# The MLP of a decoder block by Strassen's algorithm, in two phases over DRAM, and an output projection with 512 columns

## The chip, the core and the metric

The kernel runs on one core of a Trainium2 chip. The metric is the device time of one execution in microseconds (us): the median of several executions. In the rows PE is TensorE (matmuls), PEld its weight loads, DVE is VectorE, ACT ScalarE, POOL GpSimd, and SP SyncE, which issues the transfers (DMA) between DRAM and the on-chip memory SBUF. Matmul results land in PSUM.

## The reference, cut to what matters

```python
def reference(x, ...):                       # x: 1024 tokens x 1024 channels, float32
    h = rmsnorm(x, norm_mix_g)
    ...                                      # attention branch y_a, state-space branch y_b
    merged = sigmoid(g_a) * y_a + sigmoid(g_b) * y_b
    x = x + merged @ w_out                   # output projection, 1024 x 1024
    h2 = rmsnorm(x, norm_mlp_g)
    x = x + square(relu(h2 @ w_up)) @ w_down # MLP, hidden width 4096
    return rmsnorm(x, norm_final_g)
```

## The kernel before, in words

Every float32 product is made of three matmuls. Each operand is split into a rounded part "hi" (a cast on ACT) and the rest "lo" (operand minus hi, a subtraction on DVE or POOL), and `mm3` (L112 to L117) adds hi by hi, lo by hi and hi by lo into one PSUM tile. The helper `weights` loads a weight tile of 128x1024 into `raw` (two buffers) and makes `w` (four buffers) of it: hi on ACT (L108), lo on DVE unless a caller names POOL (L109).

The attention, the state-space branch and the merge gates take the first part of the program. The last stage, `st3`, has three parts, and the change is in them.

- **Gates and merge.** The tiles `mT` (hi and lo of the merged channels) are made from three projections (`ps_v`).
- **Output projection.** Four column blocks `c` of 256; for each, eight blocks `b` of 128 tokens; for each, eight channel blocks of three matmuls into `ps_o`: 768 matmuls of 256 columns. DVE adds `ps_o` to the residual `xr[b]` (L960). After the fourth column block `norm2` makes `h2T`, the normalized tokens turned round by PE transposes (`pt`, L132), split in hi and lo (L133, L134) for one half of the tokens at a time.
- **MLP.** For each of 16 pairs of hidden blocks (128 wide), `up` makes the hidden values of both token halves: 24 matmuls of 512 columns into `ps_up`, then Relu on ACT (L975), square on DVE (L976), hi on ACT (L977), lo on DVE (L978). `down` then adds the pair's part to the output: for 8 token blocks and 2 column halves 6 matmuls of 512 columns into `ps_dn`, and DVE adds that to `xr` (L995). `up` of a pair is written ahead of `down` of the pair before. Hidden values never leave SBUF. That is 1536 matmuls up and 1536 down. The last token blocks are normalized with `gfin` (L1009, L1013) and stored (L1010, L1014).

All loads and stores are issued by SP in one order; within each engine instructions run in the order that the scheduler of the language set at build time. An engine waits where its next instruction waits, and a load waits for its buffer.

Of the kernel before, what the change touches and what calls it, by code (L numbers as in the profile page):

```python
# [11 lines left out]
F32 = mybir.dt.float32  # L12
# [7 lines left out]
P = 128  # L20
# [27 lines left out]
DP1, SP1, XP1, NKQ, NVV, NQT, QL = 3, 2, 2, 2, 2, 3, 1  # L48
DENSE = 'ssksmkcssscsabasbmmmm'
# [10 lines left out]
def f32(ap):  # L60
    return ap.bitcast(F32)
# [3 lines left out]
def hybrid_block(ctx: ExitStack, tc: tile.TileContext, a: dict, out: bass.AP, dbg=None):  # L65
# [10 lines left out]
    gain = cpool.tile([P, 2, KD], F32, name="gain")  # L76
# [18 lines left out]
    mg_d = [dtile([P, S], f"mg_d{i}") for i in range(16)]  # L95

# [75 lines left out]
    with ExitStack() as st1:  # L172
# [13 lines left out]
        def norm(half, xs4, each=None):  # L186
            for xb in xs4:
                rstd = rms_rows(tp, xb, hT[7][:, :, 512:1024])
                V.tensor_scalar(xb, xb, rstd, None, op0=ALU.mult)
            transpose_norm(tp, [(dps, "d", DP1)] * 3 + [(xps, "x", XP1)] * XN, xs4, gain[:, 0], [t[:, :, half * 512:half * 512 + 512] for t in hT], each)  # L190
# [679 lines left out]
    with ExitStack() as st3:  # L870
        dps = st3.enter_context(tc.tile_pool(name="dps3", bufs=4, space=PSUM))
        mpool = st3.enter_context(tc.tile_pool(name="mpool", bufs=8))
        ep = st3.enter_context(tc.tile_pool(name="ep", bufs=5))
# [3 lines left out]
        def e4(name, shape=(P, S)):  # L877
            return ep.tile(list(shape), F32, name=name, tag="e4")

# [18 lines left out]
        mT = []  # L898
        for fp in range(4):
            wg = weights(wpool, a["w_gate"][fp], S)  # L900
            wv = weights(wpool, a["w_val"][fp], S)
            wa = weights(wpool, a["w_ab"][fp], S)
            for i in range(2):
# [4 lines left out]
                m = operand(f"mT{f}")  # L908
                for h in range(2):
                    hs = slice(h * 512, h * 512 + 512)  # L910

                    def proj(w, x):
                        ps = dps.tile([P, 512], F32, name="ps_v", tag="d")
                        mm3(ps, [(w[:, 0, k * 256 + i * P:k * 256 + (i + 1) * P],
                                  w[:, 1, k * 256 + i * P:k * 256 + (i + 1) * P],
                                  x[k][:, 0, hs], x[k][:, 1, hs]) for k in range(4)])
                        return ps


                    tg = ep.tile([P, 512], F32, name="tg", tag="r", bufs=2)  # L920
                    A.activation(tg, proj(wg, yT), AF.Tanh, scale=0.25)
                    V.scalar_tensor_tensor(tg, tg, 1.0, proj(wv, yT), op0=ALU.add, op1=ALU.mult)
                    V.scalar_tensor_tensor(tb[:, hs], tb[:, hs], 1.0, tg, op0=ALU.add, op1=ALU.mult)
                    V.scalar_tensor_tensor(ta[:, hs], ta[:, hs], 1.0, proj(wa, aT), op0=ALU.add, op1=ALU.mult)
                    V.scalar_tensor_tensor(ta[:, hs], tb[:, hs], 0.25, ta[:, hs], op0=ALU.mult, op1=ALU.add)
                    A.activation(m[:, 0, hs], ta[:, hs], AF.Copy, scale=0.5)
                    V.scalar_tensor_tensor(m[:, 1, hs], ta[:, hs], 0.5, f32(m[:, 0, hs]),
                                           op0=ALU.mult, op1=ALU.subtract)
                mT.append(m)
        xr = []  # L930
        for b in range(NB):
            if b % 2 == 0:
                x2 = mpool.tile([P, 2, S], F32, name="x2", tag="m")
            xr.append(x2[:, b % 2, :])
            nc.sync.dma_start(xr[b], a["x"][b * P:(b + 1) * P, :])
        h2T = []

        def norm2(half):
            xs4 = []
            for j in range(4):  # L940
                b = half * 4 + j
                rstd = rms_rows(ep, xr[b], e4("junk").rearrange("p (e d) -> p e d", e=2))
                xs = e4("xs")
                V.tensor_scalar(xs, xr[b], rstd, None, op0=ALU.mult)
                xs4.append(xs)

            pool, tag = ((mpool, "m"), (oppool, "opT"))[half]
            h2T.append([t[:, i] for t in (pool.tile([P, 2, 2, 512], F32R, name=f"h2T{half}{k}", tag=tag) for k in range(4))
                        for i in range(2)])
            transpose_norm(ep, [(dps, "p", P3)], xs4, gain[:, 1], h2T[half])  # L950

        for c in range(4):
            ws = [weights(wpool, a["w_out"][c, j], S) for j in range(2)]
            for b in range(NB):
                bs = slice(b * P, b * P + P)
# [24 lines left out]
        def up(i):  # L980
            wa = [(weights(wpool, a["w_up"][i + j], S), actT[(i + j) % 4]) for j in range(2)]
            for h in range(2):
                for w, act in wa:
                    up_half(w, act, h)
            return [act for _, act in wa]

        def down(i, acts, last):
            ws = [weights(wpool, a["w_down"][2 * i + j], S) for j in range(2)]
            for b in range(NB):
                bs = slice(b * P, b * P + P)  # L990
                for c in range(2):
# [25 lines left out]
        for i in range(16):  # L1017
            cur = up(2 * i)
            if prev is not None:
                down(i - 1, prev, False)  # L1020
# [75 lines left out]
```

## Time and profile before

| | |
|---|---|
| median of 3 executions | 1619.19 us (1619.05 to 1619.24) |
| profiled execution | 1618.58 us |
| its span, first to last instruction | 1616.9 us |
| PE busy | 1590.8 us, 8658 instructions |
| DVE, ACT, POOL busy | 971.0, 579.7, 152.9 us |
| DRAM traffic | 104.76 MB read, 34.60 MB written |
| output projection | 806.3 to 900.6 us |
| MLP | 900.8 to 1609.4 us |

Busy is the time in which an engine ran an instruction. Matmuls are pipelined: a row of 0.39 us starts 0.23 us after the one ahead of it, so that the time that a matmul takes from the program is the distance of two starts and not its own length. The stages of the table were read from the first and last matmul of each tile name.

### The profile page before, as it was taken

What the parts mean: (1) busy time and instruction counts of PE and PEld (TensorE: products, weight loads), DVE (VectorE), ACT (ScalarE), POOL (GpSimd) and SP (SyncE); (2) the same over time, 40 slices, a digit from 0 to 9 for tenths busy, and PEclk for the clock granted to TensorE, in tenths of its full rate; (3) what the DMA queues carried; (4) which work ended last, traced back from release to release, by engine and by line L of the source; (5) the groups of instructions that cost most, each with busy time, mean ns of one, the idle gap of its engine ahead of it and who ended that gap; (6) DMA issues with size and microseconds to landing.
All of it is one profiled execution on the core that took longest, in us unless ns stands there. A gap on an engine that the chain in (4) does not pass through costs nothing.

```text
span 1616.9 us, 22652 instructions
## 1 busy us (share of the span) xinstructions
PE 1590.8 (98%) x8658; PEld 1357.0 (84%) x8658; DVE 971.0 (60%) x1901; ACT 579.7 (36%) x1241; POOL 152.9 (9%) x254
## 2 busy tenths in 40 slices
PE   7999999999999999999999999999999999999998
PEld 5789899888888888888899888888888888888886
DVE  7995977278888887655523554444444544544446
ACT  6344443367677676522202422222211111111222
POOL 3123544210100000000000000000000000000001
PEclk9999999999999999999999999999999999999999
DMA  6335365632122111833331111111111111011102
GB/s 230 124 106 177 113 203 155 207 101 59 56 84 87 50 50 47 289 107 109 102 120 53 40 52 53 53 53 47 45 41 51 53 52 52 29 51 52 53 27 104
DMA packets 81980, 142.93 MB, mean 88 GB/s; under 512 B 12112, under 2 KB 46928, under 8 KB 81872
## 3 DMA queue, kind: packets, MB, share of 16 engines
q1 hardware_dynamic: 81872, 141.49, 27.3%
q8 instruction: 68, 1.11, 0.3%
q14 instruction: 40, 0.33, 0.1%
HBM read 104.76 MB, written 34.60 MB: 86 GB/s over the span
## 4 chain that ended last, share of the span: by engine, by line
PE 91%; DVE 6%; issue 1%; ACT 1%; DVEq 0%; POOLq 0%; ACTq 0%
PE ps_m L147 10%; PE ps_up L115 7%; PE ps_up L117 7%; PE ps_up L116 7%; PE ps_dn L115 7%; PE ps_dn L116 7%; PE ps_dn L117 7%; PE s_ps L760 4%; PE pt L801 4%; PE ps_v L117 3%; PE ps_v L115 3%; PE ps_v L116 3%; PE o_ps L711 2%; PE o_ps L712 2%; PE ps_o L117 2%; PE ps_o L116 2%
## 5 line engine op out<-in xcount | busy, mean ns | idle before, releaser
L995 DVE TENSOR_TENSOR x<-x,ps_dn 128x512 f32<-128x512 f32 x256 | 174.7, 687 | 132.5 <-PE ps_dn L117 132.4
L108 ACT CAST w<-raw 128x1024 fp32r<-128x1024 f32 (+1 forms) x114 | 118.0, 1050 | 343.3 <-PE ps_dn L117 266.1
L147 PE MATMUL ps_m<-hT,w 128*128 128x512 f32 x768 | 215.1, 400 | 0.4 <-ACT mst L153 0.3
L115 PE MATMUL ps_up<-h2T,w 128*128 128x512 f32 x512 | 201.0, 393 | 0.9 <-ACT h2T L133 0.9
L116 PE MATMUL ps_up<-h2T,w 128*128 128x512 f32 x512 | 200.6, 392 | 0.0
L117 PE MATMUL ps_up<-h2T,w 128*128 128x512 f32 x512 | 200.1, 393 | 0.0
L116 PE MATMUL ps_dn<-w,actT 128*128 128x512 f32 x512 | 199.7, 390 | 0.0
L115 PE MATMUL ps_dn<-w,actT 128*128 128x512 f32 x512 | 199.6, 390 | 0.0
L117 PE MATMUL ps_dn<-w,actT 128*128 128x512 f32 x512 | 199.4, 390 | 0.0
L976 DVE TENSOR_TENSOR r<-r 128x512 f32<-128x512 f32 x64 | 44.3, 692 | 194.2 <-ACT r L975 194.1
L147 PEld LDWEIGHTS ps_m<-hT,w 128*128 128x128 f32 x768 | 130.6, 188 | 21.5 <-ACT mst L153 0.8
L109 DVE TENSOR_TENSOR w<-raw,w 128x1024 fp32r<-128x1024 f32 x87 | 105.0, 1221 | 25.5 <-ACT w L108 25.5
L975 ACT ACTIVATE r<-ps_up 128x512 f32<-128x512 f32 x64 | 38.2, 598 | 225.2 <-PE ps_up L117 224.1
L115 PEld LDWEIGHTS ps_up<-h2T,w 128*128 128x128 f32 x512 | 96.1, 188 | 22.3 <-ACT h2T L133 1.2
L116 PEld LDWEIGHTS ps_up<-h2T,w 128*128 128x128 f32 x512 | 96.2, 188 | 21.5
L117 PEld LDWEIGHTS ps_up<-h2T,w 128*128 128x128 f32 x512 | 95.9, 188 | 21.6
L115 PEld LDWEIGHTS ps_dn<-w,actT 128*128 128x128 f32 x512 | 96.1, 188 | 20.6
L117 PEld LDWEIGHTS ps_dn<-w,actT 128*128 128x128 f32 x512 | 96.1, 188 | 20.4
L116 PEld LDWEIGHTS ps_dn<-w,actT 128*128 128x128 f32 x512 | 96.1, 188 | 20.2
L124 POOL TENSOR_TENSOR rstd<-ss,neghalf 128x1 f32<-128x1 f32 x23 | 12.6, 550 | 993.3 <-DVE ss L122 993.3
L766 ACT ACTIVATE p<-s_ps,sst 128x640 f32<-128x640 f32 (+7 forms) x128 | 90.1, 707 | 23.5 <-PE pt L801 13.4
L109 POOL TENSOR_TENSOR w<-raw,w 128x1024 fp32r<-128x1024 f32 (+1 forms) x27 | 71.3, 2643 | 162.5 <-ACT w L108 162.5
(1383 smaller groups left out, 3293.9 us busy)
## 6 DMA issues: line engine op xcount, KB each, us to landing
raw<-w_up SPq DMA_DIRECT2D x32, 512.0 KB
raw<-w_down SPq DMA_DIRECT2D x32, 512.0 KB
raw<-w_mg SPq DMA_DIRECT2D x16, 512.0 KB
mg_d<-mst SPq DMA_DIRECT2D x32, 256.0 KB
qT<-q_d SPq DMA_DIRECT2D x16, 384.0 KB
xb<-x SPq DMA_DIRECT2D x8, 512.0 KB
w1r<-w_c SPq DMA_DIRECT2D x16, 256.0 KB
q_d<-qTs SPq DMA_DIRECT2D x16, 256.0 KB
```

What stands on the lines that cost most here:

```text
L108: (hi or A.copy)(w[:, 0, :], raw)
L109: (lo or V.tensor_tensor)(w[:, 1, :], raw, f32(w[:, 0, :]), op=ALU.subtract)
L115: T.matmul(ps, lhsT=wh, rhs=xh, start=first and i == 0, stop=False)
L116: T.matmul(ps, lhsT=wl, rhs=xh, start=False, stop=False)
L117: T.matmul(ps, lhsT=wh, rhs=xl, start=False, stop=last and i == n - 1)
L147: m = T.matmul(ps, lhsT=w[:, e, ks], rhs=hT[k][:, r, hs], start=k == 0 and i == 0, stop=k == KD - 1 and i == 2)
L760: T.matmul(s_ps[:, o:o + hi - lo], lhsT=qT[:, 2 + hp * 2 + j, :], rhs=kT[g, br, hf][:, e, lo - hf * 512:hi - hf * 512], start=e == 0, stop ...
L766: A.activation(pp[j][:, 0:w], row, AF.Exp, scale=-1.0, bias=st[:, 0, j:j + 1], accum_out=st[:, 2, j:j + 1])
L801: T.transpose(pt[:, i, j, :], c[hp, br][j][:, (i0 + i) * P:(i0 + i + 1) * P], ident)
L975: A.activation(r, ps, AF.Relu)
L976: V.tensor_tensor(r, r, r, op=ALU.mult)
L995: V.tensor_tensor(xr[b][:, cs], xr[b][:, cs], ps, op=ALU.add)
```

## The change

The two products of the MLP are made by Strassen's algorithm in the form with 7 block products and 15 block sums in place of 8 block products. For a product of a 2x2 arrangement of blocks A with one of blocks B, sums S1 to S4 of A's blocks and T1 to T4 of B's are made, seven products of them, and the results are sums of those.

- **Output projection**: two column blocks of 512, 384 matmuls of 512 columns into `ps_o`.
- **norm2** now runs for one block of 128 tokens at a time after the second column block: `xs` is the row times rstd and gain (`gm`, L977), transposed into `pt`, copied to `hb`, and turned into the operands B11 and B21 (tokens 0 to 511) or B22, T1 and T2 (tokens 512 to 1023) with their hi and lo (L969, L998, L1001). `x` after the projection goes to DRAM (`x_d`). T3 and T4 are made later from whole tiles (`late_operands`: three subtractions each in `tt`, two buffers, L1011 to L1013; lo on POOL).
- **Up phase**: 16 steps `q`, each with the weights of a pair of hidden blocks. Four weight sums `sa`, `sb` (L1067 to L1071) and three weight tiles split with lo on POOL; 7 products of 12 matmuls into `pa`, `pb`, `pc`. The two products that need no weight sum (`up_open`) of the first three steps are put ahead. The squared blocks and their sums (`e1`, `e2`, `ts`) are stored to `act_d`, 1.75 MiB for a step.
- **Down phase**: seven products `op`, each over 16 `q`. For each (op, q) a part of `act_d` (one load for two q) and a block of `w_down` (or a sum T of blocks) are split (two casts on ACT, one lo on POOL and one on DVE) and multiplied by 12 matmuls, summed over q in four PSUM tiles. `x_d` is loaded back to add to.

In total 1344 matmuls up and 1344 down, each of 512 columns.

```diff
+        def norm2(b):
+            js = slice(b % 4 * P, b % 4 * P + P)
+            xs = e4("xs")
+            rstd = rms_rows(ep, xr[b], xs.rearrange("p (e d) -> p e d", e=2))
+            V.scalar_tensor_tensor(xs, xr[b], rstd, gm, op0=ALU.mult, op1=ALU.mult)
+            nc.sync.dma_start(x_d[b], xr[b])
+            hb = e4("hb", (P, 2, 4, P))
...
+                    T.transpose(pt[:, k, :], xs[:, (kh * 4 + k) * P:(kh * 4 + k + 1) * P], ident)
+                A.copy(hb[:, kh], pt)
+            if b < 4:
...
+                split_to("B11", js, hb[:, 0])
+                split_to("B21", js, hb[:, 1], G)
+                return
...
+            t1 = hb[:, 0]
+            for e in range(2):
+                V.tensor_tensor(t1, t1, f32(ops_["B11"][e][:, :, js]), op=ALU.subtract)
+            split_to("B22", js, hb[:, 1], G)
+            split_to("T1", js, t1)
+            V.tensor_tensor(hb[:, 1], hb[:, 1], t1, op=ALU.subtract)
+            split_to("T2", js, hb[:, 1])
+        def late_operands():
...
+            for k in range(4):
+                for name, x, y, eng in (("T3", "T2", "B11", V), ("T4", "B21", "T2", V)):
...
+                    t = s4("tt", (P, 512))
+                    eng.tensor_tensor(t, xh, yh, op=ALU.subtract)
+                    eng.tensor_tensor(t, t, xl, op=ALU.add)
+                    eng.tensor_tensor(t, t, yl, op=ALU.subtract)
+                    h, l = ops_[name]
+                    A.copy(h[:, k], t)
+                    G.tensor_tensor(l[:, k], t, f32(h[:, k]), op=ALU.subtract)
...
+        def up_open(q, raw0):
+            w = weights(wpool, None, S, lo=G.tensor_tensor, raw=raw0)
+            pa, pb = acc("pa"), acc("pb")
+            e1 = e4("e1", (P, 2, 512))
+            prod(pa, w[:, :, 0:512], "B11", True)
+            A.copy(e1[:, 0], pa)
+            prod(pb, w[:, :, 512:1024], "B21", True)
+            V.tensor_tensor(e1[:, 0], e1[:, 0], pb, op=ALU.add)
+            square(e1[:, 0])
+            return pa, e1
+        def up_rest(q, raw0, raw1, pa, e1):
...
+            V.tensor_tensor(s1, a21, a22, op=ALU.add)
+            V.tensor_tensor(s2, s1, a11, op=ALU.subtract)
+            wa = weights(wpool, None, S, lo=G.tensor_tensor, raw=sa)
+            V.tensor_tensor(s3, a11, a21, op=ALU.subtract)
+            V.tensor_tensor(s4_, a12, s2, op=ALU.subtract)
+            wb = weights(wpool, None, S, lo=G.tensor_tensor, raw=sb)
+            wc = weights(wpool, None, 512, lo=G.tensor_tensor, raw=a22)
+            e2 = e4("e2", (P, 2, 512))
+            pc = acc("pc")
+            prod(pa, wa[:, :, 0:512], "T2", False)
+            A.copy(e2[:, 0], pa)
+            prod(pc, wa[:, :, 512:1024], "T1", True)
+            A.copy(e2[:, 1], pc)
+            prod(pa, wb[:, :, 0:512], "T3", False)
+            V.tensor_tensor(e2[:, 1], e2[:, 1], pa, op=ALU.add)
+            square(e2[:, 1])
+            prod(pc, wb[:, :, 512:1024], "B22", False)
+            V.tensor_tensor(e2[:, 0], e2[:, 0], pc, op=ALU.add)
+            square(e2[:, 0])
+            prod(pa, wc, "T4", False)
...
+            nc.sync.dma_start(d[:, 0:2, q % 2], e1)
+            nc.sync.dma_start(d[:, 2, q % 2], e2[:, 1])
+            nc.sync.dma_start(d[:, 3:7, q % 2], t)
...
+        opened = [up_open(q, up_raw(2 * q)) for q in range(NOPEN)]
+        late_operands()
+        for q in range(16):
+            raw0, raw1 = up_raw(2 * q), up_raw(2 * q + 1)
+            up_rest(q, raw0, raw1, *(opened[q] if q < NOPEN else up_open(q, raw0)))
...
+        def down(n, op, group, first, rhs, dst):
...
+            for q in range(16):
+                if q % 2 == 0:
+                    raw = wpool.tile([P, 2, 512], F32, name="raw", tag="raw", bufs=nbuf[0])
+                    nc.sync.dma_start(raw, act_d[q // 2][:, op])
+                t = rhs(q)
+                w = wpool.tile([P, 2, 2, 512], F32R, name="w", tag="w", bufs=nbuf[1])
+                A.copy(w[:, 0, 0], raw[:, q % 2])
+                G.tensor_tensor(w[:, 0, 1], raw[:, q % 2], f32(w[:, 0, 0]), op=ALU.subtract)
+                A.copy(w[:, 1, 0], t)
+                V.tensor_tensor(w[:, 1, 1], t, f32(w[:, 1, 0]), op=ALU.subtract)
...
+        def rhs_t2(q):
+            x, t, b22 = xy[q // 2][:, q % 2, 0], xy[q // 2][:, q % 2, 1], zload(q, 1, 1)
+            V.tensor_tensor(t, b22, t, op=ALU.subtract)
+            V.tensor_tensor(x, t, x, op=ALU.subtract)
+            return t
...
+        down(0, A11, 0, True, rhs_b11, (0, c1))
+        down(1, S1, 1, True, rhs_t1, (1, c2))
+        down(2, S2, 0, False, rhs_t2, (0, c2))
+        down(3, S4, 1, False, lambda q: z[q // 4][:, q % 4], (0, c2))
+        down(4, S3, 0, False, lambda q: xy[q // 2][:, q % 2, 0], (1, c2))
+        down(5, A12, 1, True, lambda q: zload(q, 1, 0), (0, c1))
+        down(6, A22, 0, False, rhs_t4, (1, c1))
```

DVE at the start of the MLP, before: the splits of the second token half (`h2T`, L134) stand between the squares and lo parts of the first hidden blocks.

```order
L944 TENSOR_SCALAR xs<-x_9078,rstd 128x1024
L976 TENSOR_TENSOR r<-r 128x512 x2
L134 SCALAR_TENSOR_TENSOR h2T_10077<-pt,gain,h2T_10077 128x512 x2
L134 SCALAR_TENSOR_TENSOR h2T_10078<-pt,gain,h2T_10078 128x512 x2
L134 SCALAR_TENSOR_TENSOR h2T_10079<-pt,gain,h2T_10079 128x512 x2
L134 SCALAR_TENSOR_TENSOR h2T_10080<-pt,gain,h2T_10080 128x512
L978 TENSOR_TENSOR actT_10139<-r,actT_10139 128x512
```

DVE at the same place in the changed kernel, first at the second token half: T_9605 is T1's lo, T_9607 T2's lo, B_9394 and B_9395 B11's hi and lo, x_9272 the last token block's rows.

```order
L1035 TENSOR_TENSOR x_9272<-x_9272,ps_o 128x512
L998 TENSOR_TENSOR hb<-hb,B_9394 128x512
L998 TENSOR_TENSOR hb<-hb,B_9395 128x512
L125 TENSOR_SCALAR ss<-ss 128x1
L977 SCALAR_TENSOR_TENSOR xs<-x_9217,rstd,gm 128x1024
L969 TENSOR_TENSOR T_9605<-hb,T_9604 128x4x128
L1001 TENSOR_TENSOR hb<-hb 128x512
L969 TENSOR_TENSOR T_9607<-hb,T_9606 128x4x128
```

The last addition of the projection stands ahead of all work on tokens 512 to 1023, and of each of the four blocks five such operations are made. At the end of that work come the 24 subtractions of `late_operands`, of which these are the last, and then the first weight sums:

```order
L1011 TENSOR_TENSOR tt<-T_9606,B_9394 128x512
L1012 TENSOR_TENSOR tt<-tt,T_9607 128x512
L1011 TENSOR_TENSOR tt<-B_9396,T_9606 128x512
L1013 TENSOR_TENSOR tt<-tt,B_9395 128x512
L1012 TENSOR_TENSOR tt<-tt,B_9397 128x512
L1013 TENSOR_TENSOR tt<-tt,T_9607 128x512
L1067 TENSOR_TENSOR sa<-raw 128x512
L1068 TENSOR_TENSOR sa<-sa,raw 128x512
L1070 TENSOR_TENSOR sb<-raw 128x512
L1071 TENSOR_TENSOR sb<-raw,sa 128x512
```

So `sa`, from which the weights of the first product with T2 are made, stands behind all of T1 to T4. On PE the matmuls between the last `ps_o` and that product are the 72 of the three opened steps, with 32 transposes among them.

SP's transfers before, in the MLP: loads of weights alone, in pairs.

```order
L965 DMA gfin<-g_fin 128x1024
L102 DMA raw<-w_up 128x1024 x2
L102 DMA raw<-w_down 128x1024 x2
L102 DMA raw<-w_up 128x1024 x2
L102 DMA raw<-w_down 128x1024 x2
```

SP's transfers in the changed kernel where the up phase ends: act_d_161 to act_d_168 are the eight pairs of steps, of which the first down product reads one for two `q`. First from the second pair on:

```order
L1138 DMA raw<-act_d_162 128x1024
L1117 DMA gfin<-g_fin 128x1024
L1178 DMA xy<-w_down 128x512 x6
L1138 DMA raw<-act_d_163 128x1024
L1178 DMA xy<-w_down 128x512 x3
L1097 DMA act_d_168<-e_11845 128x512
L1178 DMA xy<-w_down 128x512 x5
L1115 DMA y_11923<-x_d_153 128x1024
```

Seven more loads of `x_d` follow, and behind them:

```order
L1138 DMA raw<-act_d_164 128x1024
L1098 DMA act_d_168<-ts 128x4x512
L1178 DMA xy<-w_down 128x512 x5
L1138 DMA raw<-act_d_165 128x1024
L1178 DMA xy<-w_down 128x512 x13
L1178 DMA z<-w_down 128x512 x13
L1138 DMA raw<-act_d_166 128x1024
L1178 DMA z<-w_down 128x512 x3
L1138 DMA raw<-act_d_167 128x1024
```

The loads of `act_d`, which the running product needs one after the other, stand among loads that the second and the third product or the end of the phase need: 4 MiB of `x_d` ahead of act_d_164, and 26 blocks of `w_down` (0.25 MiB each) between act_d_165 and act_d_166.

## Rows read from the trace of the kernel before

**Rows 1.** The page: span, busy time and instructions, and the chain's shares.

```profile
span 1616.9 us, 22652 instructions
PE 1590.8 (98%) x8658; PEld 1357.0 (84%) x8658; DVE 971.0 (60%) x1901; ACT 579.7 (36%) x1241; POOL 152.9 (9%) x254
PE 91%; DVE 6%; issue 1%; ACT 1%; DVEq 0%; POOLq 0%; ACTq 0%
```

**Rows 2.** Windows of the MLP: stretch, length, busy (count) by engine, clock, DMA.

```profile
1100.00:1200.00 100.00, 100.00 (x439) 82.21 (x439) 47.75 (x64) 20.30 (x28) 0.00 (x0) 1.00 0.17 53
1300.00:1400.00 100.00, 100.00 (x440) 82.13 (x439) 48.70 (x66) 19.14 (x27) 0.00 (x0) 1.00 0.17 53
```

**Rows 3.** Timeline of PE in the output projection: start, us, engine, line, operation.

```profile
829.77 0.28 PE L117 MATMUL ps_o<-w,mT 128*128 128x256 f32 x1
...
831.55 0.28 PE L117 MATMUL ps_o<-w,mT 128*128 128x256 f32 x1
```

**Rows 4.** Timeline of PE around the start of the MLP.

```profile
900.76 0.39 PE L115 MATMUL ps_up<-h2T,w 128*128 128x512 f32 x1
...
915.20 0.50 PE L115 MATMUL ps_up<-h2T,w 128*128 128x512 f32 x1 [0.94 <-ACT h2T L133]
...
920.35 1.47 PE L132 MATMUL pt<-ident,xs 128*128 128x128 f32 x12
921.58 0.48 PE L117 MATMUL ps_up<-h2T,w 128*128 128x512 f32 x1
```

**Rows 5.** Groups by line and form: busy, mean ns, idle time ahead and its releasers.

```profile
L109 DVE TENSOR_TENSOR w<-raw,w 128x1024 fp32r<-128x1024 f32 x87 | 105.0, 1221 | 25.5 <-ACT w L108 25.5
L108 ACT CAST w<-raw 128x1024 fp32r<-128x1024 f32 x110 | 113.6, 1048 | 343.3 <-PE ps_dn L117 266.1 <-PE ps_o L117 52.4 <-DMA raw<-w_out 10.6
L109 POOL TENSOR_TENSOR w<-raw,w 128x1024 fp32r<-128x1024 f32 x23 | 58.7, 2554 | 139.0 <-ACT w L108 139.0
L733 POOL TENSOR_TENSOR pc<-pc,st 128x256 f32<-128x256 f32 x16 | 9.8, 613 | 1.2
L976 DVE TENSOR_TENSOR r<-r 128x512 f32<-128x512 f32 x64 | 44.3, 692 | 194.2 <-ACT r L975 194.1
L977 ACT CAST actT<-r 128x512 fp32r<-128x512 f32 x64 | 39.6, 621 | 21.4 <-DVE r L976 21.2
L1013 DVE SCALAR_TENSOR_TENSOR x<-x,rstd,gfin 128x1024 f32<-128x1024 f32 x7 | 9.0, 1279 | 0.0
```

**Rows 6.** Timeline of POOL, then of DVE, in the same stretch.

```profile
61.95 4.68 POOL L109 TENSOR_TENSOR w<-raw,w 128x1024 fp32r<-128x1024 f32 x1 [32.49 <-ACT w L108]
67.41 2.49 POOL L109 TENSOR_TENSOR w<-raw,w 128x1024 fp32r<-128x1024 f32 x1 [0.78 <-ACT w L108]
...
62.41 0.68 DVE L254 TENSOR_TENSOR bt__632<-bXY,fim 128x512 f32<-128x512 f32 x1
63.02 0.75 DVE L494 TENSOR_TENSOR vv<-vv,vt 128x576 f32<-128x576 f32 x1
63.68 0.68 DVE L254 TENSOR_TENSOR B<-B,bt__632 128x512 f32<-128x512 f32 x1
64.40 3.23 DVE L505 TENSOR_TENSOR wq<-B,pi 128x512 f32<-128x512 f32 x1
67.66 2.79 DVE L506 TENSOR_TENSOR wq<-wq,wq 128x512 f32<-128x512 f32 x1
```

**Rows 7.** Windows with heavy transfers (the last two columns: DMA share, GB/s).

```profile
12.00:16.00 4.00, 3.79 (x15) 2.76 (x14) 3.84 (x6) 3.86 (x7) 2.87 (x1) 1.00 1.03 411
655.00:685.00 30.00, 30.00 (x131) 24.34 (x130) 22.69 (x17) 17.34 (x15) 0.00 (x0) 1.00 0.91 321
```

**Rows 8.** Timeline of PE after its first idle time, then windows behind its last matmul.

```profile
13.75 0.80 PE L115 MATMUL ps_u<-hT,w 128*128 128x512 f32 x1
14.34 0.63 PE L116 MATMUL ps_u<-hT,w 128*128 128x512 f32 x1
14.76 0.57 PE L115 MATMUL ps_u<-hT,w 128*128 128x512 f32 x1
15.17 0.39 PE L117 MATMUL ps_u<-hT,w 128*128 128x512 f32 x1
15.40 0.39 PE L115 MATMUL ps_u<-hT,w 128*128 128x512 f32 x1
...
1609.40:1612.00 2.60, 0.00 (x0) 0.00 (x0) 2.16 (x4) 1.21 (x4) 0.69 (x2) 1.00 0.46 186
1613.00:1614.00 1.00, 0.00 (x0) 0.00 (x0) 0.73 (x2) 0.00 (x0) 0.00 (x0) 0.50 0.46 184
```

More of the change, by code (lines that the diff above doesn't have):

```diff
@@ L95, in hybrid_block @@
     mg_d = [dtile([P, S], f"mg_d{i}") for i in range(16)]
+    x_d = [dtile([P, D], f"x_d{b}") for b in range(NB)]
+    act_d = [dtile([P, 7, 2, 512], f"act_d{i}") for i in range(8)]
     def operand(name):
@@ L897, in hybrid_block @@
             aT.append(o)
-        mT = []
+        mT = [[oppool.tile([P, 2, 2, 512], F32R, name=f"mT{h}{k}", tag="opT") for k in range(4)] for h in range(2)]
         for fp in range(4):
@@ L1016, in hybrid_block, with op2 @@
-        prev = None
[L1017 to L1020, printed above, removed]
-            prev = cur
-        down(15, prev, True)
+                    ssm_part(i, h)
+                    if fp < 3:
+                        attn_part(i, h)
+            if fp == 3:
+                for i in range(2):
+                    for h in range(2):
+                        attn_part(i, h)
+        ops_ = {}
+        def op2(name, pool, tag):
+            ops_[name] = [pool.tile([P, 4, 512], F32R, name=f"{name}{e}", tag=tag) for e in range(2)]
@@ new lines, in prod @@
+        def prod(ps, w, name, first):
+            h, l = ops_[name]
+            for k in range(4):
+                ks = slice(k * P, k * P + P)
+                for i, (e, x) in enumerate(((0, h), (1, h), (0, l))):
+                    T.matmul(ps, lhsT=w[:, e, ks], rhs=x[:, k], start=first and k + i == 0, stop=k == 3 and i == 2,
+                             skip_group_check=not first)
+        def up_open(q, raw0):
[8 more added lines that the diff above has]
+            return pa, e1
@@ new lines, in hybrid_block, with mms @@
+        gfin = e4("gfin")
+        nc.sync.dma_start(gfin, a["g_fin"])
+        A11, A12, A22, S1, S2, S3, S4 = range(7)
+        xy, z = [], []
+        groups = ([acc(f"pg{i}") for i in range(4)],
+                  [acc("pg4"), dps.tile([P, 512], F32, name="pg5", tag="p", bufs=2),
+                   dps.tile([P, 512], F32, name="pg6", tag="p", bufs=2), mps.tile([P, 512], F32, name="pg7", tag="d")])
+        c1, c2 = slice(0, 512), slice(512, 1024)
+        def down(n, op, group, first, rhs, dst):
+            ps = groups[group]
+            held = []
+            def mms(q, w, b):
+                bs = slice(b * P, b * P + P)
+                for i, (e, r) in enumerate(((0, 0), (1, 0), (0, 1))):
+                    T.matmul(ps[b], lhsT=w[:, 0, e, bs], rhs=w[:, 1, r], start=first and q + i == 0,
+                             stop=q == 15 and i == 2, skip_group_check=not first)
+            for q in range(16):
[8 more added lines that the diff above has]
+                V.tensor_tensor(w[:, 1, 1], t, f32(w[:, 1, 0]), op=ALU.subtract)
+                if n == 6 and q >= 12:
+                    held.append((q, w))
+                    continue
+                for b in range(4):
+                    mms(q, w, b)
+            r, cs = dst
+            for b in range(4):
+                for q, w in held:
+                    mms(q, w, b)
+                yb = y[r * 4 + b][:, cs]
+                V.tensor_tensor(yb, yb, ps[b], op=ALU.add)
+                if n >= 5:
+                    final(r * 4 + b, cs)
```

234 lines of the change are left out of this document (134 added, 100 removed).

## The prediction

> **What bounds the kernel now.** I read the page first: PE is busy for 1590.8 of 1616.9 us and holds 91% of the chain of work that ended last, so time comes out only where PE has less to do, and goes in only where PE is made to wait [rows 1]. Then the windows of the MLP: 100 us hold 439 or 440 matmuls of 512 columns, PE is busy in all of it, DVE for about 48 us, ACT for 20, POOL for nothing, and transfers move 53 GB/s [rows 2]. One such matmul is therefore worth 100/439.5 = 0.2275 us of the program, and everything else in the MLP has slack today. Last the timeline of PE where the MLP starts: it waited 0.94 us there once, for the split of the second token half, and twelve transposes took 1.23 us, 0.10 each [rows 4]. The other engines had no work that PE had to stand for.
>
> **The change, part by part.** The sum is made against the profiled execution of 1618.6 us; the median is 0.6 above that.
>
> *Products of the MLP.* 3072 matmuls become 2688 of the same shape: 384 x 0.2275 = 87.4 us less (87.3 to 87.5 by the two windows).
>
> *Output projection.* In the timeline 15 starts of 256 columns lie 1.78 us apart, 0.1187 us each [rows 3]: 768 x 0.1187 = 91.2 us. Of 512 columns there are 384, at 0.2275 87.4 us: 3.8 us less. The transposes are 64 in both.
>
> *Start of the MLP.* Before's own wait of 0.94 us goes. What comes is a wait for DVE. By the order, after DVE's last addition of `ps_o` and up to the second weight sum of `sa`, from which the first product with T2 is made, DVE has 52 operations of 128x512, 3 squares of that size and 3 of 128x1024 (rows times rstd and gain). By the nearest groups, 692 ns and 1279 ns [rows 5], that is 55 x 0.69 + 3 x 1.28 = 41.8 us; back to back such operations start some 0.64 apart (63.02 to 63.68 was 0.66 [rows 6]), which makes it 39. The cast of `sa` on ACT (1.05) is behind them; its lo on POOL (2.55) is wanted only one matmul later [rows 5]: 3.6 more. PE has in this time 72 opened matmuls and 32 transposes: 72 x 0.2275 + 32 x 0.10 = 19.6 us. PE so stands for 39 + 3.6 - 19.6 = 23 us if nothing disturbs DVE.
>
> Something does. In one stretch of an earlier stage POOL's subtraction of 128x1024 took 4.68 us in place of 2.4 while three DVE operations of 0.68 to 0.75 ran, then DVE's next one took 3.23 us, until POOL was done, and the one after it 2.79 beside POOL's next of 2.49. From 61.95 to 70.45, 8.5 us, the two did work that alone takes about 2 x 2.4 for POOL and 5 x 0.7 for DVE, 8.3: they took turns [rows 6]. In the MLP before, POOL has no work [rows 2], so that DVE never paid for this; now it has. At the start POOL makes the lo of B22 in four pieces and of T3 and T4 in eight, each of 512 elements a row. No row has that size; it lies between 0.61 us for 256 and 2.55 for 1024 [rows 5], and I take half of the latter: 12 x 1.28 = 15.3, and two or three weight lo's of 2.55 fall in as well, 5: 20 us, which DVE loses. Without turns the wait is 23, with all of them 43, and if DVE also sits through the way from rstd to the transposes and back for a block or two, 50. I take **43**, since the rows show turns wherever both ran.
>
> [...]
>
> *Up phase, steady.* A step is 84 matmuls, 19.1 us. DVE has 15 operations of 0.69 in it, 10.4; POOL three lo's of 2.55 and one of 1.28, 8.9; ACT three casts of 1.05 and a few of 0.62, 6.2; transfers 2.75 MiB. [...] I take no wait here, and keep the other for a rival.
>
> *End of up, start of down.* SP's transfers run one behind the other at about 0.37 MiB/us (388 GB/s, between 411 and 321 [rows 7]). Each (op, q) gives PE 12 matmuls, 2.73 us. The first `xy` tiles lie where B22 lay, which is read until one product ahead of the end of the up phase. From there 9.25 MiB stand ahead of act_d_164 (1.5 of `xy`, gfin, two parts of act_d, 4 MiB of `x_d`, the last stores, 2 more of `xy`): 25 us, against six `q` and the last product and its lead, 16.4 + 4.6: a wait of 4. To act_d_165 it is 2.75 MiB, 7.4 us against two `q` of 5.5: 2. To act_d_166 it is 7 MiB, 18.9 against 5.5: 13.4. Together **19**; at 411 GB/s (0.392 MiB/us) 16.5, at 321 (0.306) 30.
>
> *Down phase, steady.* DVE has one to three operations for a (op, q) and POOL one: 1.28 + 0.69 = 2.0 in turns, and in the product with T2 1.28 + 3 x 0.69 = 3.35 against 2.73. That is 0.62 x 16 = 10 too much, of which four `w` buffers filled ahead take some 7: **3** (0 to 10). The tail behind the last matmul is the same chain of square, rstd, scaling and store as before: nothing.
>
> *Clock.* [...] And at the program's start the first matmuls after idle time lay 0.59, 0.42 and 0.41 us apart, then 0.23 [rows 8]. The four long waits above will each be followed by some work at about half rate. One costs at least 0 and by that start, 0.7 for three matmuls and something for the transposes ahead of them, up to 4. I take 1.5 each: **6** (0 to 16).
>
> The sum: 1618.6 - 87.4 - 3.8 - 0.9 + 43 + 19 + 3 + 6 = 1597.5, and 0.6 for the median: **1598 us**.
>
> **Rivals.**
> - *Waits are covered* (DVE and POOL hardly take turns in these instructions, and transfers go at 411 GB/s): 23 at the start, 16.5 at the transition, none in down, no clock: 1618.6 - 92.1 + 39.5 + 0.6 = 1567. For it: POOL's rows in turns are of 1024 elements, and there were only a few. Against: every pair that met shows it. Chance 0.22.
> - *The up phase loops on DVE and POOL*: all 15 operations take turns, and waits between them make a step 20.1 in place of 19.1: 16 more, 1614; with slow transfers (30) up to 1622. For it: 19.3 against 19.1. Chance 0.18.
> - *Slower*: POOL's subtraction of 128x512, which no row has, costs what one of 128x1024 costs, 2.4. Then a (op, q) of down needs 2.4 + 0.69 = 3.1 in turns, 0.37 over PE's 2.73, 112 times: 41 more, 1639. It decides from (1619.2 - 1598)/112 = 0.19 over, that is POOL at 2.23. Against: POOL's time falls with the size, 0.61 for 256 elements, so that 512 should stand near 1.25 [rows 5]. Chance 0.09.
> - That the change doesn't save the matmuls is no case for me: the new ones have the shape of the old, and the number is fixed by the program.
>
> The forecast, waits of 85 down to 60 us in all, 1588 to 1612, has the remaining 0.51.
>
> **How the numbers follow.** A difference of 0.2%, 3.2 us, is about what a measurement of this kernel can tell from no change. The forecast and the covered case are faster (0.73); of the up-phase case 0.11 is faster and 0.07 the same; the last is slower, 0.09. The range leaves out a part of the covered case and the slower one: 1566 to 1626.
>
> **What would show it.** Right: PE's windows in the up phase full but for its start, with the first T2 product some 60 us after the last `ps_o`; DVE operations of 2 us and more beside POOL's; gaps of PE on `act_d` loads behind the first eight `q` of down, the longest ahead of q 10. Wrong: POOL at 1.2 us with DVE at 0.69 beside it (then 1567), or PE windows of under 95 in the middle of up or down (then 1614 and more), or no gap at the transition, if the transfers were begun earlier than I let them.

## The result, and the profile after

The changed kernel takes 1640.49 us (median of four, 1637.73 to 1641.72) against 1619.2: a ratio of 1.0129, 95% interval 1.0112 to 1.0147. It is slower by 1.3%, above the range of the prediction. The profiled execution is the 1637.73 one; before's was 1618.58.

The page after, as in [rows 1] (span, busy, chain):

```profile
span 1636.0 us, 22261 instructions
PE 1527.2 (93%) x7890; PEld 1276.1 (78%) x7890; DVE 1135.0 (69%) x1927; ACT 678.9 (42%) x1443; POOL 487.5 (30%) x446
PE 66%; DVE 17%; DMA 9%; issue 3%; ACT 2%; POOL 1%; SPq 1%; DVEq 0%; POOLq 0%; ACTq 0%
```

PE has 768 instructions less and is busy for 63.6 us less, but its share of the chain fell from 91% to 66%: DVE (17%) and transfers (9%) now set part of the end. Three groups by tile give the stages, each with its first and last start; `pg` are the sums of the down phase:

```profile
L120 PE MATMUL ps_o<-w,mT x128: 389/393/480, 806.9 to 898.6; 128*128 128x512 f32 x128
L1045 PE MATMUL pa<-T,w x576: 387/393/796, 960.3 to 1291.5; 128*128 128x512 f32 x192
L1132 PE MATMUL pg<-w x1344: 387/389/796, 1292.9 to 1625.7; 128*128 128x512 f32 x192
```

And windows of the three stages, as in [rows 2]:

```profile
898.90:960.30 61.40, 23.69 (x105) 18.71 (x103) 48.91 (x61) 22.41 (x39) 24.62 (x18) 0.70 0.11 34
960.30:1291.70 331.40, 308.70 (x1272) 245.65 (x1272) 237.94 (x224) 88.72 (x122) 149.38 (x63) 0.96 0.41 138
1292.90:1627.10 334.20, 313.07 (x1344) 253.69 (x1344) 224.34 (x234) 135.71 (x252) 156.94 (x116) 0.97 0.46 157
```

Against the work of PE in each, by the prediction's own prices: the **start** took 61.4 us, of which 19.6 are matmuls and transposes: 42 lost. The **up phase** took 332.6 (960.3 to the first `pg` at 1292.9) for 1344 - 72 = 1272 matmuls, 1272 x 0.2275 = 289.4: 43 lost. The **down phase** took 333.0 for 1344, at 0.2267 (794 in 180 us of its undisturbed part) 304.7: 28 lost. The tail behind the last matmul is 10.1 us in place of 7.5. The waits of PE (total, times, longest):

```profile
PE pa L1045 <- ACT w L111: 29.0, 1, 29.0
PE pa L1045 <- DVE e L1081: 21.5, 11, 3.1
PE pg L1132 <- ACT w L1141: 17.0, 3, 12.3
...
PE pt L983 <- DVE xs L977: 7.6, 2, 5.9
PE pg L1132 <- DVE w L1144: 2.4, 1, 2.4
```

Of these rows the first and the fourth are the start, the third and the fifth the transition. The second came 11 times, in nearly every step of the up phase, and is the one that the prediction did not have. The chain of one such step, in order of time:

```profile
1104.19 0.37 SPq L1098
...
1104.66 6.50 DMA raw<-w_up
...
1111.86 0.69 DVE sb L1070
...
1113.79 0.69 DVE e L1081
1114.48 0.02 issue
1114.51 2.78 DVE e L1061
1117.29 0.61 DVE e L1084
...
1117.92 2.18 DVE e L1061
...
1120.82 1.70 DVE ts L1093
...
1123.12 2.83 DVE e L1088
...
1125.98 0.70 DVE ts L1094
...
1126.69 0.37 SPq L1098
...
1127.17 6.51 DMA raw<-w_up
```

It is a loop that never passes PE. DVE ends the last sum in `ts`; SP issues its store (L1098) and only then the load of the next weights, which it has behind the store in its order; the load lands 6.5 us later; DVE, which waited for it (5.77 us in the timeline, ahead of `sa`), makes the weight sums, then the addition from `pa` (L1081) that PE waits for, then squares and sums up to `ts`. From 1104.66 to 1127.17 it is 22.5 us, against 19.1 of matmuls. For the 13 steps behind the three opened ones that would be 13 x 3.4 = 44 us, as much as the whole loss of the up phase; the first experiment shows how much of it the loop really costs. Behind five of the eleven waits (2.35, 2.41, 2.45, 2.45 and 3.05 us) the twelve matmuls that follow take 4.2 to 4.5 us at a mean clock of 0.62 to 0.66; behind the other six (0.96 to 2.46 us) they take 2.9 at 1.00. PE's windows around the one of 2.45 us in this step (busy, clock, transfers):

```profile
1112.00:1113.00 1.00, 0.07 (x1) 1.00 0.00 0
1113.00:1114.00 1.00, 0.00 (x0) 1.00 0.00 0
...
1115.00:1116.00 1.00, 1.00 (x4) 0.50 0.74 262
1116.00:1117.00 1.00, 1.00 (x3) 0.50 0.62 238
```

The granted clock is 0.50 behind the wait, but since the chain of the loop has no row of PE, that should cost nothing more here (argued from the chain; no run kept PE busy through the wait). At the transition PE's timeline has the waits one by one:

```profile
1292.90 8.89 PE L1132 MATMUL pg<-w 128*128 128x512 f32 x38 [1.00 <-ACT w L1143]
1304.19 8.01 PE L1132 MATMUL pg<-w 128*128 128x512 f32 x34 [2.40 <-DVE w L1144]
1316.50 7.17 PE L1132 MATMUL pg<-w 128*128 128x512 f32 x24 [4.30 <-ACT w L1141]
1324.03 1.21 PE L1132 MATMUL pg<-w 128*128 128x512 f32 x4 [0.36 <-ACT w L1141]
1325.93 4.84 PE L1132 MATMUL pg<-w 128*128 128x512 f32 x20 [0.69 <-POOL w L1142]
1343.07 2.50 PE L1132 MATMUL pg<-w 128*128 128x512 f32 x5 [12.30 <-ACT w L1141]
```

The groups ahead of 1316.50 hold 38 + 34 = 72 matmuls, six `q`: that is the wait for act_d_164. Behind it come 24, 4 and 20, four more, so that the last is the wait for act_d_166.

### The profile page after: what moved, and what is told of

Read it like the earlier page. It is cut to its first block, busy times and chain, and to the rows that moved or that the text cites. A ratio compares the mean times of both kernels' runs of the same rounds, so it can differ in the third digit from the quotient of the medians.

```text
span 1636.0 us, 22261 instructions
## 1 busy us (share of the span) xinstructions
PE 1527.2 (93%) x7890; PEld 1276.1 (78%) x7890; DVE 1135.0 (69%) x1927; ACT 678.9 (42%) x1443; POOL 487.5 (30%) x446
## 4 chain that ended last, share of the span: by engine, by line
PE 66%; DVE 17%; DMA 9%; issue 3%; ACT 2%; POOL 1%; SPq 1%; DVEq 0%; POOLq 0%; ACTq 0%
PE pg L1132 17%; PE ps_m L150 10%; DMA raw<-w_up 5%; PE s_ps L763 4%; PE pt L804 4%; DVE e L1061 3%; PE ps_v L120 3%; PE ps_v L118 3%; PE ps_v L119 3%; PE o_ps L714 2%; PE pa L1045 2%; PE o_ps L715 2%; DMA xy<-w_down 2%; PE ps_o L120 2%; PE ps_o L118 2%
## 5 line engine op out<-in xcount | busy, mean ns | idle before, releaser
L1132 PE MATMUL pg<-w 128*128 128x512 f32 x1344 | 313.1, 394 | 21.1 <-ACT w L1141 17.0
L1132 PEld LDWEIGHTS pg<-w 128*128 128x128 f32 x1344 | 253.7, 190 | 80.5 <-ACT w L1141 18.2
L1142 POOL TENSOR_TENSOR w<-raw,w 128x512 fp32r<-128x512 f32 x112 | 155.7, 1393 | 179.3 <-ACT w L1141 179.3
L1045 PE MATMUL pa<-T,w 128*128 128x512 f32 x576 | 152.8, 417 | 51.7 <-ACT w L111 29.0
L112 POOL TENSOR_TENSOR w<-raw,w 128x1024 fp32r<-128x1024 f32 (+2 forms) x59 | 141.8, 2411 | 172.2 <-ACT w L111 172.2
L1045 PEld LDWEIGHTS pa<-T,w 128*128 128x128 f32 x576 | 114.2, 200 | 83.9 <-ACT w L111 29.4
L150 PEld LDWEIGHTS ps_m<-hT,w 128*128 128x128 f32 x768 | 130.6, 188 | 21.5 <-ACT mst L156 0.8
L1144 DVE TENSOR_TENSOR w<-xy,w 128x512 fp32r<-128x512 f32 x64 | 71.4, 1124 | 63.6 <-ACT w L1143 54.1
L111 ACT CAST w<-raw 128x1024 fp32r<-128x1024 f32 (+2 forms) x82 | 79.0, 967 | 51.4 <-DMA raw<-w_out 15.7
L769 ACT ACTIVATE p<-s_ps,sst 128x640 f32<-128x640 f32 (+7 forms) x128 | 90.1, 708 | 23.5 <-PE pt L804 13.4
L763 PE MATMUL s_ps<-kT,qT 128*128 128x512 f32 (+3 forms) x384 | 85.8, 337 | 0.2
L804 PE MATMUL pt<-ident,p 128*128 128x128 f32 x528 | 83.8, 275 | 2.1 <-DVE pl__5079 L708 0.9
L766 DVE CUSTOM_DVE_ANT_0 s_ps<-s_ps,cmask 128x256 f32<-128x256 f32 (+7 forms) x96 | 63.9, 677 | 19.6 <-PE s_ps L763 19.1
L1061 DVE SCALAR_TENSOR_TENSOR e<-e 128x512 f32<-128x512 f32 x48 | 75.2, 1566 | 1.4
L119 PE MATMUL ps_a<-w,hT 128*128 128x256 f32 (+1 forms) x256 | 74.7, 292 | 0.0
L118 PE MATMUL ps_a<-w,hT 128*128 128x256 f32 (+1 forms) x256 | 74.5, 291 | 0.0
L120 PE MATMUL ps_a<-w,hT 128*128 128x256 f32 (+1 forms) x256 | 74.0, 289 | 0.0
```

The costliest lines, as they stand in the source:

```text
L118: T.matmul(ps, lhsT=wh, rhs=xh, start=first and i == 0, stop=False)
L119: T.matmul(ps, lhsT=wl, rhs=xh, start=False, stop=False)
L120: T.matmul(ps, lhsT=wh, rhs=xl, start=False, stop=last and i == n - 1)
L150: m = T.matmul(ps, lhsT=w[:, e, ks], rhs=hT[k][:, r, hs], start=k == 0 and i == 0, stop=k == KD - 1 and i == 2)
L763: T.matmul(s_ps[:, o:o + hi - lo], lhsT=qT[:, 2 + hp * 2 + j, :], rhs=kT[g, br, hf][:, e, lo - hf * 512:hi - hf * 512], start=e == 0, stop ...
L804: T.transpose(pt[:, i, j, :], c[hp, br][j][:, (i0 + i) * P:(i0 + i + 1) * P], ident)
```

## The experiments

Nine kernels, of which seven have a single execution and the last two, with all or most of the edits, the median of four. The last `ps_o` starts at 898.5 to 901.3 us in them, up to 2.8 us apart though nothing ahead of the MLP was changed, so gains are read from the stage concerned and not from the total alone. First the up phase. **The stores on ACT:**

```diff
-            nc.sync.dma_start(d[:, 0:2, q % 2], e1)
+            nc.scalar.dma_start(d[:, 0:2, q % 2], e1)
...
-            nc.sync.dma_start(d[:, 3:7, q % 2], t)
+            nc.scalar.dma_start(d[:, 3:7, q % 2], t)
```

> The changed kernel, with the 48 stores to act_d issued by ACT in place of SP. Theory (queue order): in the up phase the weight sums wait for w_up loads that SP issues only after the store of ts, 1 MiB, and that land 6.5 us after it; a step is 22.5 us by that loop. With the stores elsewhere the loads go out as soon as their buffer is free: a step of about 19.1 to 19.6 us, PE's waits on the addition from pa (21.5 us) gone, and with them most of the time at the lower clock; up phase from the first T2 product on 331 down to 290 to 300, in all about 1600. Rival (turns alone): DVE and POOL are the loop, whatever the loads do: step 22 us, in all 1633 to 1640.

Measured 1606.42 us, a little above the 1600 of the theory: the up phase took 300.4 us in place of 332.6. A window of it:

```profile
1060.00:1080.00 20.00, 20.00 (x88) 16.21 (x87) 16.32 (x17) 6.01 (x9) 9.18 (x4) 1.00 0.48 169
```

PE is full, its wait for L1081 is gone, and yet DVE is still busy for 16.3 of the 20 us, and for 226 us of the phase against 238 before: the turns are there but no longer on the path. Queue order holds; turns alone fall. The run also says how much of the 43 us was the loop: 32. Most of the other 11 stay with PE full: the matmuls of the up phase start 0.2316 us apart in this window, not 0.2275, which is 5 us over 1272 (why is open), and the first 24 with T1 and T2, behind the long wait of the start, take 9.8 us in place of 5.6. **POOL's lo parts out of the up phase:**

```diff
+        def lo_copy(o, r, h, op):
+            A.copy(o, r)
...
-            w = weights(wpool, None, S, lo=G.tensor_tensor, raw=raw0)
+            w = weights(wpool, None, S, lo=lo_copy, raw=raw0)
```

(and the same for `wa`, `wb`, `wc`.)

> The changed kernel, with the lo parts of the up phase's weights not computed by POOL's subtraction but filled by a copy on ACT (part of the product is so left out: lo is not operand minus hi). POOL then has nothing to do in the steady up phase, and DVE no turns to take. Theory (one loop, of queue order and turns): DVE's stretch from the addition from pa to the last sum, 12.9 us, falls to about 6 to 7, the loop from 22.5 to below PE's 19.1, so that this too brings the up phase from 331 to 290 to 300 and the whole to about 1600. Rival (the loads' 6.5 us behind the store alone, or the transfers' volume): step stays 21 to 22.5, in all 1630 or more. Rival (ACT becomes the bound with 3.7 us more of copies): step above 20.

Measured 1600.62 us, up phase 296.5. The stores were still on SP. What changed on DVE, first in the changed kernel, then here (mean ns of one):

```profile
L1061 DVE SCALAR_TENSOR_TENSOR e<-e 128x512 f32<-128x512 f32 x48 | 75.2, 1566 | 1.4
L1091 DVE TENSOR_TENSOR ts<-e 128x512 f32<-128x512 f32 x16 | 30.5, 1908 | 0.5
L1081 DVE TENSOR_TENSOR e<-e,pa 128x512 f32<-128x512 f32 x16 | 10.9, 682 | 5.9 <-PE pa L1045 5.9
```

```profile
L1064 DVE SCALAR_TENSOR_TENSOR e<-e 128x512 f32<-128x512 f32 x48 | 34.2, 713 | 1.1
L1094 DVE TENSOR_TENSOR ts<-e 128x512 f32<-128x512 f32 x16 | 12.1, 759 | 0.4
```

The square (L1061, here L1064) went from 1566 to 713 ns, the first sum of `ts` from 1908 to 759, and DVE's busy time in the phase from 238 to 147 us: 5.7 us for each of 16 steps. Taken from a loop of 22.5 that would leave 16.8, an estimate, below PE's 19.1. But the run does not show that this alone frees PE, because SP's order came out another way at build time. In the changed kernel both loads of a step stand behind the store of `ts`; here one of them stands ahead of both stores:

```profile
1066.98 0.33 SPq L105 DMA_DIRECT2D raw<-w_up  x1
1070.55 0.37 SPq L1099 DMA_DIRECT2D act_d<-e  x1
1072.36 0.37 SPq L1101 DMA_DIRECT2D act_d<-ts  x1
1073.73 0.34 SPq L105 DMA_DIRECT2D raw<-w_up  x1
```

In every step of the phase at least one load has come ahead of the store of `ts`, and on DVE the next step's weight sum starts at 1070.44, ahead of the last sum of `ts` at 1071.64. So the loop is open in its order as well as shorter. The kernel with the stores on ACT shows that the order alone is enough; that the turns alone are enough is not shown.

The start. **The subtractions for T3 and T4 behind the first weight sums:**

```diff
-        late_operands()
...
             wc = weights(wpool, None, 512, lo=G.tensor_tensor, raw=a22)
+            if q == 0:
+                late_operands()
```

> The changed kernel, with the 24 subtractions for T3 and T4 written behind the weight sums and splits of the first step in place of ahead of them. Theory (DVE's order at the start of the MLP makes the wait of 42 us): by DVE's order 28 operations of 0.66, 3 of 1.28 and some 8 us of turns stand before the first T product now, 30 to 34 us against PE's 19.6: a wait of 11 to 15, and later one of about 15 for T3; in all 1638 - 16 = about 1622. Rival (the wait is for the loads of the first weights or for POOL's lo's, not for these subtractions): no change, 1636 to 1640.

Measured 1636.52 us: by the total no change, as the rival had it, but not for its reason. The first product with T2 now starts 41.6 us after the last `ps_o` in place of 61.5, 20 us sooner, with one with T1 ahead of it; but the phase from there to the first `pg` grew from 332.6 to 347.6. PE's waits say where it went:

```profile
PE pt L983 <- DVE xs L977: 13.6, 2, 8.8
PE pa L1045 <- ACT T L1015: 11.2, 3, 4.6
PE pa L1045 <- POOL T L1016: 1.8, 3, 0.6
```

PE now stands for T3 and T4 themselves. The order only chooses which product waits; the work on DVE and POOL between the last `ps_o` and T4 is what costs. **POOL's part in it:**

```diff
-            (lo or V).tensor_tensor(l[:, :, js], src, f32(h[:, :, js]), op=ALU.subtract)
+            if lo is None:
+                V.tensor_tensor(l[:, :, js], src, f32(h[:, :, js]), op=ALU.subtract)
+            else:
+                A.copy(l[:, :, js], src)
...
-                    G.tensor_tensor(l[:, k], t, f32(h[:, k]), op=ALU.subtract)
+                    A.copy(l[:, k], t)
```

> Stores on ACT, and the lo parts that POOL makes at the start of the MLP (B21, B22, T3, T4) filled by a copy on ACT in place of POOL's subtraction (lo is so not operand minus hi there; part of the product is left out). Theory of the prediction (20 of the 42 us of the wait are turns of DVE and POOL): wait down to about 22, in all 1586. Rival (turns are a smaller part, waits for POOL's results through the two tt buffers and the chain from rstd to xs the rest; DVE's own work in that stretch, 48.9 us busy of 61.4, is most of it): wait 28 to 36, in all 1592 to 1600.

Measured 1591.04 us against 1606.42 of the kernel with the same stores. The first T product starts 47.6 us after the last `ps_o` in place of 61.4. The window, as above:

```profile
899.79:947.35 47.56, 24.07 (x106) 19.12 (x104) 42.36 (x61) 29.01 (x51) 7.02 (x6) 0.73 0.13 45
```

The twelve lo parts of this stretch are so worth 14 us. The prediction had 15.3 for them; the other 5 of its 20 are weight lo's, which POOL still makes in this run (its 7.0 us are three of these and three rstd). A wait of 28 is left, at the rival's edge, and that is the prediction's 23 and 5. What was taken away is only half turns: DVE's busy time fell from 48.9 to 42.4, 6.5 us, and its idle time from 12.5 to 5.2, 7.3 us, much of it the waits for POOL's results through `tt` (four waits for L1016 of 1.15 to 1.43 us, 4.9 in all, in the changed kernel). **Fewer subtractions** (T2 - B11 is B22 - B12):

```diff
+            t3 = s4("t3", (P, 4, P))
+            V.tensor_tensor(t3, hb[:, 1], t1, op=ALU.subtract)
+            split_to("T3", js, t3, G)
             for e in range(2):
                 V.tensor_tensor(t1, t1, f32(ops_["B11"][e][:, :, js]), op=ALU.subtract)
...
+            t4 = s4("t4", (P, 4, P))
+            V.tensor_tensor(t4, f32(ops_["B21"][0][:, :, js]), hb[:, 1], op=ALU.subtract)
+            V.tensor_tensor(t4, t4, f32(ops_["B21"][1][:, :, js]), op=ALU.add)
+            split_to("T4", js, t4, G)
...
-        late_operands()
```

> The kernel with the stores on ACT, and T3 computed as B22 - B12, which it equals, and T4 as B21 - T2, both for each block of 128 tokens in norm2 from the float32 tile: 4 + 8 operations of 128x512 on DVE in place of 24, none of them behind the two tt buffers that wait for POOL. Theory (the wait of 42 us at the start is DVE's and POOL's work in turns): 12 operations of 0.66 and the 4 x 2.2 us that DVE waited for POOL and took turns fall away: 42 to about 26, in all 1588 to 1594. Rival (as with the moved subtractions, where the wait only went to another place): less than 6 off, 1600 or more.

Measured 1594.06 us, 12.4 below the kernel with the stores on ACT and at the upper end of what was expected; the start took 48.8 us in place of 61.4, which leaves a wait of 29 where 26 was expected. Work taken away shortens it, where work moved did not.

The transition. **More buffers for act_d, x_d written later:**

```diff
-                    raw = wpool.tile([P, 2, 512], F32, name="raw", tag="raw", bufs=nbuf[0])
+                    if q % 6 == 0:
+                        raw = wpool.tile([P, 2, 512], F32, name="raw", tag="raw", bufs=nbuf[0])
+                    else:
+                        raw = e4("raw", (P, 2, 512))
...
+                if n == 0 and q == 10:
+                    for i in range(4):
+                        y2 = mpool.tile([P, 2, S], F32, name="y2", tag="m")
```

> The changed kernel, with the act_d loads of the down phase in up to six buffers (the four free ones of e1's pool beside the two) in place of two, and the loads of x_d written in the middle of the first down product in place of ahead of it. Theory (transfers wanted later stand ahead of act_d loads on SP): the first act_d loads now go out ahead of most of them, and the loss of 28 us at the transition falls to 5 to 12: in all 1615 to 1622. Rival (the transition is limited by the volume that the first product needs, 8 MiB and the last stores): loss stays above 20, in all 1630 or more.

Measured 1635.05 us, a miss for the theory in size: the down phase itself took 325.5 us, 7.5 less, but began with a wait of 3.45. Its longest wait, 9.0 us at 1339, is again for an act_d load, behind these transfers on SP (start, time of the whole group):

```profile
1332.85 8.39 SPq L1182 DMA_DIRECT2D z<-w_down  x12
1341.58 1.73 SPq L1142 DMA_DIRECT2D raw<-act_d  x3
```

The loads of `x_d` had gone out early all the same: SP issued the eight from 1301.68 on, 4 us behind the first matmul of the phase (1297.67), and q 10, at which they are written, starts at 1327.34. Six buffers did not settle volume against order. **Later loads held back** (each behind a one-column copy that waits for the running product's `w`; on the kernel with the stores on ACT):

```diff
+        def ahead(n, q, w1):
+            if n == 0:
+                t = xy[q // 2][:, q % 2, 1]
+                A.copy(t[:, 0:1], w1)
+                wd(q, 0, 1, t)
+            if n == 0 and q in (4, 6, 8, 10) or n == 1 and q in (0, 2, 4, 6):
...
+                A.copy(y[b][:, 0:1], w1)
+                nc.sync.dma_start(y[b], x_d[b])
+            if n == 1:
...
+                A.copy(t[:, 0:1], w1)
+                wd(q, 1, 1, t)
```

> The kernel with the stores on ACT (1606.4, of which the down phase lost 28.6 us at its start), and the loads of x_d, of the blocks for T1 and of the blocks for T2 each written one product ahead of their use and held back by a one-column copy on ACT that waits for the running product's weights. Theory (order of transfers: those of later products stand ahead of act_d loads): the loss falls to 5 to 12, in all 1583 to 1592. Rival (volume: the transfers of the first product, 14 MiB with the held ones, fill the channel in any order): loss above 20, 1598 or more.

Measured 1585.95 us. The down phase took 311.9 us in place of 332.1. At its start, where the changed kernel stood:

```profile
1262.00:1282.00 20.00, 19.93 (x86) 15.70 (x85) 15.76 (x19) 8.21 (x22) 9.00 (x6) 1.00 1.03 386
```

The transfers still fill the channel (a share of 1.03, 386 GB/s) and PE is full beside them: it was the order, not the volume. The 7 us that are left are short gaps in the first 100 us, where 20 us hold 78 to 87 matmuls and later 89 or 90. **All of it together:**

> All edits together: stores on ACT, T3 and T4 in norm2, act_d loads in up to six buffers, the other down loads one product ahead and held back. If the three losses (up loop 42, start 42, transition 28) are separate, the gains add: 1606 - 16 - 20 = 1570, 1562 to 1580, faster than before's 1619. If they share a cause or one takes over from another, it stays above 1585.

Measured 1580.12 us (1579.58 to 1581.81), ratio 0.9758 to before (0.9742 to 0.9775). That is just above the range for gains that add; they do, but for 6 us: with act_d in six buffers a wait of 3.9 and three of 3.4 in all came back at the transition. So, **without the six buffers:**

> Stores on ACT, T3 and T4 in norm2, and the later down loads held back, but act_d loads in two buffers as at first (with six of them a wait of 3.9 and one of 2.2 us stood at the transition, where with two there was 1.0 in all). If the gains of the separate runs add: 1606.4 - 20.5 - 12.4 = 1573.5, 1571 to 1577; if the six buffers were no loss, 1579 to 1582 again.

Measured 1576.71 us (1576.1 to 1577.85), ratio 0.9738 (0.9722 to 0.9754): faster than both kernels, 2.6% below before. The total lies within the range, near its upper end; the up phase took 302.5 and the down phase 313.0, each about what the separate runs had. Its busy times:

```profile
PE 1516.5 (96%) x7890; PEld 1270.1 (81%) x7890; DVE 1116.4 (71%) x1915; ACT 683.4 (43%) x1483; POOL 483.2 (31%) x446
```

## Why the prediction was wrong

It failed in one step: "I take no wait here", of the up phase. It set DVE's and POOL's sums beside PE's 19.1 us and the 2.75 MiB of a step beside the channel, and found room in each, which was right: DVE is busy for 16 us of a step of 22.5, POOL for 10, and the channel for 0.41 of the phase. No run of the changed kernel shows the 0 that the sum has for it; in its place PE waited 11 times for L1081, 21.5 us, and the step above took 22.5. What it did not do is to follow what waits for what from one step to the next. SP's order has the next weights behind the store of `ts`, and the store's data are the last that DVE makes of a step, so that the resources, each free for part of a step, stand in one ring. Its rival for the up phase (DVE's 10.4 and POOL's 8.9 us in turns, 19.3 against 19.1) put 16 us on the two; the phase lost 43, of which the ring is 32 by the edit on SP that opens it alone. The edit on POOL, which shortens DVE's part and changes SP's order too, gave 36 back. Of the prediction's own signs of being wrong this is the one that came: PE is busy for 92.5 us from 1100 to 1200, under its 95. The misses of the other steps nearly cancel, so that the up phase is about the whole of the 40 us between 1598 and 1638.

The other steps, in the order of the sum:

- **Products of the MLP** (87.4): close. The count of a window takes in matmuls that stand across its ends, so that 0.2275 is a little low: by the distance of starts it was 0.2286 before (1000 to 1600), and it is 0.2316 in the undisturbed up phase and 0.2273 in the down phase. By these the change is worth 3072 x 0.2286 - 1344 x 0.2316 - 1344 x 0.2273 = 85.5.
- **Output projection** (3.8): 92.4 in place of 94.3 us, 1.9. Of the 64 transposes 32 fall into it now, and 24 did before: 0.8 of the difference.
- **Start** (43): 42. The size was right, and POOL's twelve lo parts are 14 where 15.3 stood; but the sum took them for turns, and half of them are waits. So near a hit is in part luck: in the run without them DVE is idle for 5.2 us that the sum does not have, and the way from the last sum of `sa` to the product is 1.1 in place of 3.6.
- **Transition** (19, as 4, 2 and 13.4): PE waited 4.3 us ahead of q 6, 0.36 ahead of q 8 and 12.3 ahead of q 10, and 1.0, 2.4 and 0.7 ahead of the first, within the fourth and within the ninth q, where I had none: 21 in all. That order and not volume makes them was shown by the loads held back.
- **Down, steady** (3): the products with T1 and T2, from 1380 to 1420, hold 168 matmuls where the later windows hold 180: 12 x 0.2267 = 2.7.
- **Clock** (6): the granted clock was 0.50 behind the long waits, of 29.0 us (a mean of 0.53 from 960.3 to 968.5), 4.30 (1316.5 to 1319) and 12.3 (1343.07 to 1346.5), and 1.00 behind those of 1.0 and 2.4. The cost is the rest of the losses at most: 42 less the waits of 38 at the start, 28 less 21 and 2.7 in the down phase, 4 and 4 us; in the up phase some 3 us follow the long wait of the start, and the rest is inside the ring.
- **Tail** (0): 10.1 in place of 7.5 us. The last four token blocks are finished one behind the other, each with its own squares and rstd.

With the ring opened by the stores alone the kernel measured 1606, within the range. The chance of 0.09 for slower went to another mechanism: POOL's 128x512, which that rival had at 2.4 us, took 1.39 (1.3 in the median, 112 of L1142), as the prediction itself took it.

## What to carry to other kernels

Where a loop's engines all have slack, look for a ring: follow one piece of data through a step and on into the next, through the order of the queue that issues its transfers, here with the load of the next weights behind the store of `ts`, so that it went out 0.1 us after that and the step took 22.5 us with 19.1 of matmuls. Loads that nothing held back went out ahead of what was wanted next: in the changed kernel PE stood 12.3 us for an `act_d` load that had them ahead of it. Held back by a dependence they left the down phase at 311.9 us in place of 332.1; a later place in the program did not hold them. An edit to the work of one engine can change the order of another engine's queue at build time; lay the two orders side by side before reading such a run as the test of one cause. And when work is moved and the total stays, look where the wait went before calling the theory wrong.

## What the runs showed of the hardware

In these runs DVE's turns with POOL went with where the operands lay. In the up phase of the changed kernel the additions that read PSUM (L1056, L1081, L1084) kept to 0.68 us each whether POOL ran or not, 0.69 at most, while operations with both inputs in SBUF went from 0.69 to as much as 2.9. The two squares below ended 0.55 us behind POOL's own, at 1117.29 and 1120.09 behind 1116.74 and 1119.54. These rows, of DVE in the step above, lie beside POOL's:

```profile
1114.51 2.78 DVE L1061 SCALAR_TENSOR_TENSOR e<-e 128x512 f32<-128x512 f32 x1
1117.21 0.68 DVE L1084 TENSOR_TENSOR e<-e,pc 128x512 f32<-128x512 f32 x1
1117.92 2.17 DVE L1061 SCALAR_TENSOR_TENSOR e<-e 128x512 f32<-128x512 f32 x1
```

```profile
1114.36 2.38 POOL L112 TENSOR_TENSOR w<-sa,w 128x1024 fp32r<-128x1024 f32 x1 [12.68 <-ACT w L111]
1116.70 2.84 POOL L112 TENSOR_TENSOR w<-sb,w 128x1024 fp32r<-128x1024 f32 x1
```

The addition at 1117.21 ran its 0.68 us within POOL's 2.84; the square ahead of it took 2.78 beside POOL's 2.38, where without POOL's lo parts it took 0.71 (the mean of 48).

Moving the 48 stores from SP to ACT gave 32 us in the up phase. The issues themselves are a small part of that: one of a store took SP 0.32 to 0.38 us (once 0.55), and the ring above has one of 0.37 in a step, 13 x 0.37 = 4.8 us for the 13 steps, an estimate. What was saved beside them is time in which SP, in its order, waited for the stores' data (120.8 us in the phase ahead of L1096, 15 times, up to 10.4) with a load behind them that needed nothing of it.
